# Sixteen tiles of experts on TensorE: half-column products kept together, activation behind the branch, transposes moved

## The chip, the cores and the metric

The kernel runs on one core of a Trainium2 chip. A core has TensorE (PE, with its weight loads listed as PEld), VectorE (DVE), ScalarE (ACT), GpSimd (POOL) and SyncE (SP), which run side by side and wait for each other through semaphores, and 16 DMA engines. The metric is the device time of one execution in microseconds (us).

## The reference, cut to what matters

Two blocks of a network, one after the other, on 512 tokens of width 1024. The change lies in the expert layer of the first block. 32 experts of inner width 256 stand in four groups; each token picks one group and two experts in it, with weights that come from softmaxes:

```python
for grp in range(N_GROUPS):
    sl = slice(grp * EXPERTS_PER_GROUP, (grp + 1) * EXPERTS_PER_GROUP)
    hg = jnp.einsum("td,edf->tef", ht, w_gate[sl])
    hu = jnp.einsum("td,edf->tef", ht, w_up[sl])
    act = jax.nn.silu(hg) * hu * combine[:, sl, None]
    y = y + jnp.einsum("tef,efd->td", act, w_down[sl])
```

All is in float32. The kernel computes an expert only for the tokens that picked it.

## The kernel before, in words

Before the experts, a router on the chip builds a table: 16 main tiles of 128 token places, each shared by two experts (number x and x + 16). One expert of a tile has its tokens in the first rows, the other in the last. Each has 64 rows of its own, and up to 32 more rows where it has more tokens; the flag `need[x]` says that such rows are in use in tile x. So a tile has *wide* products (64 rows for each expert, always) and *narrow* products (32 rows, under a branch on `need`).

For one tile x these steps are done (names as in the code and in the trace):

- `gather` (POOL): an indirect DMA fetches the 128 tokens' rows into `xg`; ACT scales them (`scale`, one ACTIVATE of 1,024 columns).
- `moe_xt`: 8 transposes on TensorE into two `pxt` banks, which DVE copies to `xt`.
- up: for k = 0..7 a product `moe_up` with each expert's `gu` weights, into the PSUM banks `pgA` and `pgB`. A wide product takes 64 columns of the array, and the two experts' products run at once in the two halves of the array. A float32 product shows as two matmul records in the trace, so that one k-step is two pairs of records.
- `narrow`: under a branch, the same products for the 32 more rows; in the other arm of the branch a product with a tile of zeros fills these rows.
- `moe_act`: four pieces, each a Silu on ACT and then a multiply on DVE, into `sa` and `sb`.
- `moe_st`: 4 transposes into the bank `pst`, and a DVE copy to `st`.
- `moe_down`: products of `st` with the `dn` weights into two banks `py`, again on half columns: part 0, a branch with the narrow rows, part 1. ACT copies the result rounded to `yh`, DVE subtracts for the rest, `yl`.
- `moe_hot` (DVE): `toh`, which has a one where a tile's place belongs to a token.
- `moe_back`: 8 banks `pb`, each filled by two products on full columns (`yh`, `yl` by `toh`), which return the rows to the tokens; DVE adds each bank to the residual `xT`.

The steps are skewed over the loop's iterations and stand in an order written by hand. Iteration x runs the up products of tile x; between its k-steps stand `moe_st` of tile x - 1 (behind k = 1) and the eight `moe_back` of tile x - 2 (one behind each of k = 1 to 6, two behind k = 7). Then come `narrow` and `moe_act` of x, `moe_xt` and `scale` for the next tiles, `moe_down` of x - 1, `moe_hot`, and the requests for weights. The banks `pxt`, `pst`, `py` and `pb` share a ring of four.

Weights come by SP's queue: `gu` of four transfers of 1,024 KB for each tile and `dn` of four of 512 KB. `pump`, at the end of iteration x, requests `dn` of tile x + 1 and `gu` of tile x + 3, whose buffers must be free; the rings hold three tiles of `gu` and two of `dn`.

A branch (`tc.If`) with no other arm, as in `moe_down` (L1880), is on TensorE's sequencer a COMPARE_BRANCH and, where it isn't taken, an EVENT_SEMAPHORE that does the semaphore counts that the products would have done. Behind the 16 main tiles a loop does further tiles of overfull experts.

Of the kernel before, what the change touches and what calls it, by code (L numbers as in the profile page):

```python
# [10 lines left out]
F32 = mybir.dt.float32  # L11
# [10 lines left out]
P = 128  # L22
T = 512
D = 1024
KD = 8
# [150 lines left out]
class Build:  # L176
# [1689 lines left out]
        self.nc.vector.tensor_copy(st[:, 0:2 * n], pt[:, 0:2 * n * P].rearrange("p (k t) -> p k t", t=P))  # L1866
        return st

    def moe_down(self, mp, st, dn, wide, narrow=(), need=None):


        pys = [self.pc("py") for _ in dn]

        def part(k, parts, start, stop):
            for py, d in zip(pys, dn):
                for i, r, n in parts:
                    self.mm(py[r:r + n], st[:, 2 * i + k, r:r + n], d[i][:, k, :], start, stop)
        part(0, wide, True, False)
        if narrow:
            with self.tc.If(need > 0):  # L1880
                for k in range(2):
                    part(k, narrow, False, False)
        part(1, wide, False, True)
        ys = []
        for py in pys:
            yh, yl = [mp.tile([P, T], F32R, tag="y", bufs=4, name=n) for n in ("yh", "yl")]
            self.act(yh, py, AF.Copy)
            self.tt(yl, py, yh.bitcast(F32), OP.subtract)
            ys.append((yh, yl))
        return ys  # L1890
# [67 lines left out]
    def moe(self, mp, pump, tab_d):  # L1958

        tab, ids = self.tab, self.ids  # L1960
        n = NMAIN
        rows = ((slice(0, 64), slice(64, 96)), (slice(32, 64), slice(64, 128))), ((slice(0, 32), slice(64, 128)), (slice(0, 64), slice(96, 128)))

        parts = ((((0, 0, 64), (1, 64, 64)), ((0, 64, 32), (1, 32, 32))), (((1, 0, 64), (0, 64, 64)), ((0, 0, 32), (1, 96, 32))))
        g, xt, ps, s, st, y, oh, need = {}, {}, {}, {}, {}, {}, {}, {}

        def scale(x):
            if x < n:
                self.act(g[x], g[x], AF.Copy, scale=tab[:, 3, x:x + 1])

        def start(x):
            if x == 0:
                scale(x)
            xt[x] = self.moe_xt(mp, g.pop(x))
            if x + 3 < n:
                g[x + 3] = self.gather(ids[:, x + 3:x + 4], x + 3)
            need[x] = self.nc.tensor.value_load(self.need[0:1, x:x + 1])
            ps[x] = [self.pd("pgA"), self.pd("pgB") if x % 2 == 0 else self.ps.tile([P, T], F32, tag="a", bufs=self.ps_a, name="pgB")]

        def narrow(x):  # L1980

            with self.tc.If(need[x] > 0) as c:
                for k in range(KD):
                    self.moe_up(ps[x], xt[x], gus, k, parts[x % 2][1])
            with c.Else():
                for i, r, m in parts[x % 2][1]:
                    self.mm(ps[x][i][r:r + m, :], self.zero[:, 0:m], self.zero)

        for x in range(3):
            g[x] = self.gather(ids[:, x:x + 1], x)  # L1990
        pump(0, 0, eng="gpsimd")
        start(0)
        scale(1)
        for x in range(n + 2):
            gus = [self.gus[x + 16 * i] for i in range(2)] if x < n else None
            for k in range(KD):
                if x < n:
                    self.moe_up(ps[x], xt[x], gus, k, parts[x % 2][0])
                if k == 1 and 0 < x <= n:
                    st[x - 1] = self.moe_st(mp, s.pop(x - 1))  # L2000
                for j in ((), range(k - 1, k), range(6, KD))[min(k, 1) + k // 7] if x > 1 else ():
                    self.moe_back(y[x - 2][j // 4], oh[x - 2], j // 4, (j % 4,))
            if x < n:
                narrow(x)
                i = x % 2
                s[x] = self.sA[i], self.sB[i]
                for e in range(2):
                    for r in rows[i][e]:
                        self.moe_act(s[x][e], ps[x][e], tab[:, 1 + e, x:x + 1], r)
                del ps[x], xt[x]  # L2010
            if x + 1 < n:
                start(x + 1)
            if x + 2 < n:
                scale(x + 2)
            if x == 0:
                self.route_extra([mp.tile([P, T], F32, tag="y", bufs=4, name="xs") for _ in range(4)])
            if x == 1:
                self.route_extra2()
                self.dma("scalar", tab_d, tab)
            if 0 < x <= n:  # L2020
                c = x - 1
                y[c] = self.moe_down(mp, st.pop(c), [[self.dns[c + 16 * e, h] for e in range(2)] for h in range(2)],
                                     *parts[c % 2], need[c])
                oh[c] = self.moe_hot(tab[:, 0, c:c + 1])
            pump(2 * (x + 1), 4 * x)

    def moe_extra(self, mp, mw, wg, wu, wd, tab_d, gu_bufs, dn_bufs):
# [773 lines left out]
```

## Time and profile before

| | |
|---|---|
| median of three runs | 2750.66 us (2750.01 to 2764.87) |
| profiled execution: its own time | 2758.55 us |
| profiled execution: span from the first to the last instruction | 2756.8 us |
| TensorE busy (whole span) | 2525.0 us, 92% |
| DVE, ACT, POOL busy (whole span) | 56%, 34%, 35% |
| main tiles of experts, first transposes to last `pb` | 780.7 to 1122 us |

The busy shares are of the whole execution; the experts are an eighth of it. What a change there does is read from the stretch itself. Times of single instructions are in us from the span's start. "[0.19 <-X]" behind an instruction is the idle time of its engine before it and what ended that. [...]

### The profile page before, as it was taken

How to read it: one execution, taken by the hardware profiler on the slowest of the kernel's cores; microseconds unless marked ns; L12 is line 12 of the kernel's file. 1: busy time of each engine (PE TensorE's matmuls, PEld its weight loads, DVE VectorE, ACT ScalarE, POOL GpSimd, SP SyncE). 2: the span in 40 equal slices, each digit the busy share in tenths (PEclk: the TensorE clock that was granted, in tenths of full speed). 3: DMA queues.
4: the chain of work that ended last, by engine and by line, in shares of the span. 5: the costliest groups of instructions: out<-in, count | busy, mean ns of one | idle time of the engine just before them, and what ended most of it. 6: DMA issues, size and time to landing. Idle time of an engine off the chain costs nothing.

```text
span 2756.8 us, 35101 instructions
## 1 busy us (share of the span) xinstructions
PE 2525.0 (92%) x13640; PEld 1836.8 (67%) x13640; DVE 1530.1 (56%) x2483; ACT 932.7 (34%) x1534; POOL 959.9 (35%) x652
## 2 busy tenths in 40 slices
PE   7887888787969999889999999999999999999999
PEld 4676776565533333557777777878756777888887
DVE  4896594344356645565465487884444345453523
ACT  3434223443212211333444332323332344442422
POOL 1454454333210000343553333344232343344443
PEclk8999998788979999999999999999999999999999
DMA  9356565634388974332445246552231225132321
GB/s 263 96 179 183 158 178 178 205 103 157 128 310 333 360 286 153 122 119 93 156 149 192 68 153 198 168 183 92 89 105 40 92 74 193 64 106 92 107 89 65
DMA packets 332300, 419.09 MB, mean 152 GB/s; under 512 B 33608, under 2 KB 275760, under 8 KB 323680
## 3 DMA queue, kind: packets, MB, share of 16 engines
q1 hardware_dynamic: 312848, 377.12, 41.6%
q10 hardware_dynamic: 14624, 25.28, 2.8%
q0 software_dynamic: 4656, 14.35, 1.6%
q8 instruction: 114, 1.87, 0.3%
q14 instruction: 58, 0.48, 0.1%
HBM read 387.66 MB, written 33.23 MB: 153 GB/s over the span
## 4 chain that ended last, share of the span: by engine, by line
PE 45%; DVE 6%; issue 3%; ACT 2%; POOL 2%; DMA 2%; ACTq 0%; POOLq 0%; DVEq 0%
PE pd L199 36%; PE psc L199 2%; DVE adacc L214 2%; PE tm L199 2%; POOL wlo L205 2%; PE ptot L199 1%; DMA raw<-in_w_up 1%; DVE cv L214 1%; PE po L199 1%; PE pc L199 1%; PE pz L199 1%; PE pso L199 1%; PE pst L199 1%; PE pn L199 1%; PE pr L199 1%
## 5 line engine op out<-in xcount | busy, mean ns | idle before, releaser
L205 POOL TENSOR_TENSOR wlo<-raw,whi 128x1024 fp32r<-128x1024 f32 (+3 forms) x317 | 721.0, 2280 | 1232.8 <-ACT whi L196 1208.9
L199 PE MATMUL pd<-h,whi 128*128 128x512 f32 (+1 forms) x3440 | 1099.4, 401 | 27.8 <-DVE stg L214 5.9
L199 PEld LDWEIGHTS pd<-h,whi 128*128 128x128 f32 x3440 | 647.4, 194 | 185.9 <-issue 26.1
L199 PE MATMUL pd<-h,wlo 128*128 128x512 f32 (+1 forms) x1720 | 676.1, 393 | 20.4 <-POOL wlo L205 20.4
L196 ACT ACTIVATE whi<-raw 128x1024 fp32r<-128x1024 f32 (+3 forms) x319 | 313.9, 993 | 265.7 <-PE pd L199 117.4
L199 PEld LDWEIGHTS pd<-h,wlo 128*128 128x128 f32 x1720 | 332.4, 193 | 93.0 <-POOL wlo L205 24.7
L199 PE MATMUL pd<-fyh,whi 128*128 128x512 f32 (+1 forms) x546 | 205.5, 376 | 10.7 <-ACT whi L196 5.2
L214 DVE SCALAR_TENSOR_TENSOR cv<-pd,vec,cv 128x511 f32<-128x511 f32 (+1 forms) x176 | 131.7, 748 | 144.0 <-ACT cv L196 138.4
L199 PE MATMUL pd<-fyh,wlo 128*128 128x512 f32 (+1 forms) x546 | 203.1, 372 | 6.0 <-POOL wlo L205 6.0
L199 PE MATMUL pd<-fyl,whi 128*128 128x512 f32 (+1 forms) x546 | 202.3, 371 | 2.5 <-DVE fyl L205 2.5
L214 DVE SCALAR_TENSOR_TENSOR adacc<-raw,cs,adacc 128x256 f32<-128x256 f32 x288 | 198.9, 691 | 9.4
L199 PE MATMUL pgB<-gu,xt 128*64 128x512 f32 (+1 forms) x304 | 154.8, 617 | 3.0 <-DVE xt L205 3.0
L214 DVE SCALAR_TENSOR_TENSOR xTl<-pd,mod,xTl 128x512 f32<-128x512 f32 (+1 forms) x73 | 49.4, 683 | 193.6 <-PE pd L199 193.6
L199 PE MATMUL pgA<-gu,xt 128*64 128x512 f32 (+1 forms) x304 | 154.9, 618 | 0.0
L199 PE MATMUL tm<-whi,h 128*128 128x256 f32 x640 | 129.5, 295 | 7.9 <-ACT whi L196 7.9
L214 DVE SCALAR_TENSOR_TENSOR xT<-pb,mod,xT 128x512 f32<-128x512 f32 x128 | 93.4, 748 | 77.0 <-PE pb L199 77.0
L199 PEld LDWEIGHTS pd<-fyh,whi 128*128 128x128 f32 x546 | 105.4, 193 | 42.0 <-ACT whi L196 11.7
L199 PEld LDWEIGHTS pd<-fyh,wlo 128*128 128x128 f32 x546 | 105.3, 193 | 24.8 <-POOL wlo L205 7.7
L199 PEld LDWEIGHTS pd<-fyl,whi 128*128 128x128 f32 x546 | 105.1, 192 | 19.5 <-DVE fyl L205 3.2
L199 PEld LDWEIGHTS tm<-whi,h 128*128 128x128 f32 x640 | 106.4, 199 | 9.2 <-ACT whi L196 8.4
L199 PE MATMUL tm<-wlo,h 128*128 128x256 f32 x320 | 93.5, 292 | 7.7 <-POOL wlo L205 7.6
L196 ACT ACTIVATE cv<-pd,vec 128x512 f32<-128x512 f32 x88 | 68.2, 775 | 95.3 <-PE pd L199 94.8
(564 smaller groups left out, 3383.4 us busy)
## 6 DMA issues: line engine op xcount, KB each, us to landing
raw<-in_ada SPq DMA_DIRECT2D x64, 1024.0 KB, 5.3
raw<-in_w_in SPq DMA_DIRECT2D x54, 1024.0 KB, 5.4
raw<-in_w_up SPq DMA_DIRECT2D x44, 1024.0 KB, 5.0
gu<-in_wg SPq DMA_DIRECT2D x30, 1024.0 KB, 8.5
gu<-in_wu SPq DMA_DIRECT2D x30, 1024.0 KB, 7.0
dn<-in_wd SPq DMA_DIRECT2D x59, 512.0 KB, 8.3
raw<-in_w_dn SPq DMA_DIRECT2D x16, 1024.0 KB, 5.2
raw<-in_wo SPq DMA_DIRECT2D x12, 1024.0 KB
```

Source lines behind the costliest of these rows:

```text
L196: return self.nc.scalar.activation(out, in_, func, **kw)
L199: return self.nc.tensor.matmul(out, lhsT, rhs, start=start, stop=stop)
L205: return (eng or self.nc.vector).tensor_tensor(out, a, b, op=op)
L214: return (eng or self.nc.vector).scalar_tensor_tensor(out, a, s, b, op0=op0, op1=op1)
```

## The change

Within an iteration the order is made anew. `moe_st` of tile x - 1 and the first four `moe_back` of tile x - 2 stand together behind k = 2. Behind k = 5 stand `moe_xt`, the gather and `scale` for the following tiles (`rows_of`), and then the other four `moe_back`. The up products of k = 6 and 7, part 0 of `moe_down` of x - 1, both branches, part 1, and the next tile's k = 0 to 2 follow each other with nothing on full columns between. The narrow up products and `moe_act` (`end_up`) are called between part 0 and the branch of `moe_down`. The branch of the up products has no other arm any more: four banks are taken once ahead of the loop, their narrow rows are filled with zeros once, and tiles of one parity use the same two banks. `moe_hot` stands ahead of `moe_down`. In the first two iterations the last pieces of the router's table (`route_extra`, `route_extra2`) are moved with it.

```diff
--- before.py
+++ after.py
@@ -1866,7 +1866,7 @@
         self.nc.vector.tensor_copy(st[:, 0:2 * n], pt[:, 0:2 * n * P].rearrange("p (k t) -> p k t", t=P))
         return st
 
-    def moe_down(self, mp, st, dn, wide, narrow=(), need=None):
+    def moe_down(self, mp, st, dn, wide, narrow=(), need=None, between=None):
 
 
         pys = [self.pc("py") for _ in dn]
@@ -1876,6 +1876,8 @@
                 for i, r, n in parts:
                     self.mm(py[r:r + n], st[:, 2 * i + k, r:r + n], d[i][:, k, :], start, stop)
         part(0, wide, True, False)
+        if between is not None:
+            between()
         if narrow:
             with self.tc.If(need > 0):
                 for k in range(2):
@@ -1968,60 +1970,62 @@
             if x < n:
                 self.act(g[x], g[x], AF.Copy, scale=tab[:, 3, x:x + 1])
 
-        def start(x):
-            if x == 0:
-                scale(x)
+        def rows_of(x):
             xt[x] = self.moe_xt(mp, g.pop(x))
             if x + 3 < n:
                 g[x + 3] = self.gather(ids[:, x + 3:x + 4], x + 3)
             need[x] = self.nc.tensor.value_load(self.need[0:1, x:x + 1])
-            ps[x] = [self.pd("pgA"), self.pd("pgB") if x % 2 == 0 else self.ps.tile([P, T], F32, tag="a", bufs=self.ps_a, name="pgB")]
-
-        def narrow(x):
-
-            with self.tc.If(need[x] > 0) as c:
+
+        def end_up(x):
+
+            with self.tc.If(need[x] > 0):
                 for k in range(KD):
                     self.moe_up(ps[x], xt[x], gus, k, parts[x % 2][1])
-            with c.Else():
-                for i, r, m in parts[x % 2][1]:
-                    self.mm(ps[x][i][r:r + m, :], self.zero[:, 0:m], self.zero)
+            i = x % 2
+            s[x] = self.sA[i], self.sB[i]
+            for e in range(2):
+                for r in rows[i][e]:
+                    self.moe_act(s[x][e], ps[x][e], tab[:, 1 + e, x:x + 1], r)
+            del ps[x], xt[x]
 
         for x in range(3):
             g[x] = self.gather(ids[:, x:x + 1], x)
         pump(0, 0, eng="gpsimd")
-        start(0)
+
+        banks = [[self.pd("pgA"), self.pd("pgB")], [self.pd("pgA"), self.ps.tile([P, T], F32, tag="a", bufs=self.ps_a, name="pgB")]]
+        for x in range(2):
+            for i, r, m in parts[x][1]:
+                self.mm(banks[x][i][r:r + m, :], self.zero[:, 0:m], self.zero)
+        scale(0)
+        rows_of(0)
         scale(1)
         for x in range(n + 2):
             gus = [self.gus[x + 16 * i] for i in range(2)] if x < n else None
+            if x < n:
+                ps[x] = banks[x % 2]
+
             for k in range(KD):
                 if x < n:
                     self.moe_up(ps[x], xt[x], gus, k, parts[x % 2][0])
-                if k == 1 and 0 < x <= n:
+                if k == 2 and 0 < x <= n:
                     st[x - 1] = self.moe_st(mp, s.pop(x - 1))
-                for j in ((), range(k - 1, k), range(6, KD))[min(k, 1) + k // 7] if x > 1 else ():
-                    self.moe_back(y[x - 2][j // 4], oh[x - 2], j // 4, (j % 4,))
-            if x < n:
-                narrow(x)
-                i = x % 2
-                s[x] = self.sA[i], self.sB[i]
-                for e in range(2):
-                    for r in rows[i][e]:
-                        self.moe_act(s[x][e], ps[x][e], tab[:, 1 + e, x:x + 1], r)
-                del ps[x], xt[x]
-            if x + 1 < n:
-                start(x + 1)
-            if x + 2 < n:
-                scale(x + 2)
+                if k == 5 and x + 1 < n:
+                    rows_of(x + 1)
+                    scale(x + 2)
+                    if x == 1:
+                        self.route_extra2()
+                        self.dma("scalar", tab_d, tab)
+                if k in (2, 5) and x > 1:
+                    self.moe_back(y[x - 2][k // 5], oh[x - 2], k // 5, range(4))
+            if 0 < x <= n:
+                c = x - 1
+                oh[c] = self.moe_hot(tab[:, 0, c:c + 1])
+                y[c] = self.moe_down(mp, st.pop(c), [[self.dns[c + 16 * e, h] for e in range(2)] for h in range(2)],
+                                     *parts[c % 2], need[c], (lambda: end_up(x)) if x < n else None)
+            elif x == 0:
+                end_up(0)
             if x == 0:
                 self.route_extra([mp.tile([P, T], F32, tag="y", bufs=4, name="xs") for _ in range(4)])
-            if x == 1:
-                self.route_extra2()
-                self.dma("scalar", tab_d, tab)
-            if 0 < x <= n:
-                c = x - 1
-                y[c] = self.moe_down(mp, st.pop(c), [[self.dns[c + 16 * e, h] for e in range(2)] for h in range(2)],
-                                     *parts[c % 2], need[c])
-                oh[c] = self.moe_hot(tab[:, 0, c:c + 1])
             pump(2 * (x + 1), 4 * x)
 
     def moe_extra(self, mp, mw, wg, wu, wd, tab_d, gu_bufs, dn_bufs):
```

## Rows read from the trace of the kernel before

**Rows 1.** One steady tile (busy of each engine, PEclk, DMA share, GB/s).

```profile
846.73:865.48 18.75, 18.56 (x80) 6.94 (x78) 11.40 (x20) 3.85 (x7) 0.99 (x1) 1.00 0.92 348
```

**Rows 2.** Waits from 780 to 1130 us (us in total, times, longest).

```profile
PE pb L199 <- DVE toh L210: 4.4, 3, 1.9
```

**Rows 3.** Timeline of PE, one tile (start, us, instructions, idle before).

```profile
845.85 0.39 PE L199 MATMUL pb<-toh,yh 128*128 128x512 f32 x1
846.08 0.40 PE L199 MATMUL pb<-toh,yl 128*128 128x512 f32 x1
...
846.73 1.16 PE L202 MATMUL pxt<-const_ident,xg 128*128 128x128 f32 x8
847.82 1.94 PE L199 MATMUL py<-dn,st 128*64 128x512 f32 x8
849.94 1.94 PE L199 MATMUL py<-dn,st 128*64 128x512 f32 x8 [0.19 <-PE py L199]
851.68 0.59 PE L199 MATMUL pgA<-gu,xt 128*64 128x512 f32 x1
...
853.53 0.51 PE L202 MATMUL pst<-const_ident,sa 128*128 128x128 f32 x2
...
854.03 0.48 PE L199 MATMUL pb<-toh,yh 128*128 128x512 f32 x1
...
854.67 0.64 PE L199 MATMUL pgA<-gu,xt 128*64 128x512 f32 x1
...
856.35 0.64 PE L199 MATMUL pgA<-gu,xt 128*64 128x512 f32 x1
...
865.48 1.16 PE L202 MATMUL pxt<-const_ident,xg 128*128 128x128 f32 x8
```

**Rows 4.** The branch L1880, 846 to 852 us (ns min/median/max, starts).

```profile
L1880 PEldq COMPARE_BRANCH  x1: 207/207/207, 847.5 to 847.5; - x1
L1880 PEldq EVENT_SEMAPHORE  x1: 51/51/51, 849.8 to 849.8; - x1
```

**Rows 5.** The branch L1880, 809 to 812 us.

```profile
L1880 PEldq COMPARE_BRANCH  x1: 213/213/213, 809.7 to 809.7; - x1
L1880 PEldq EVENT_SEMAPHORE  x1: 51/51/51, 810.9 to 810.9; - x1
```

**Rows 6.** Timeline of ACT and DVE, the same tile as in rows 3.

```profile
846.05 1.41 DVE L214 SCALAR_TENSOR_TENSOR xT<-pb,mod,xT 128x512 f32<-128x512 f32 x2 [0.92 <-PE pb L199]
...
846.83 0.37 ACT L196 ACTIVATE sa<-pgA 32x256 f32<-32x256 f32 x1 [13.01 <-PE pgB L199]
...
849.71 0.49 DVE L214 SCALAR_TENSOR_TENSOR sb<-sb,tab,pgB 32x256 f32<-32x256 f32 x1 [0.44 <-ACT sb L196]
...
851.75 0.69 DVE L205 TENSOR_TENSOR yl<-py,yh 128x512 fp32r<-128x512 f32 x1 [0.23 <-ACT yh L196]
```

**Rows 7.** Timeline of ACT, the scaling of tile 3.

```profile
811.24 1.15 ACT L196 ACTIVATE xg<-xg,tab 128x1024 f32<-128x1024 f32 x1 [2.80 <-DMA xg<-xa_d,ids]
```

**Rows 8.** Timeline of PE: first products of tiles 1 to 3.

```profile
795.82 0.64 PE L199 MATMUL pgB<-gu,xt 128*64 128x512 f32 x1 [2.96 <-DVE xt L205]
...
812.75 0.59 PE L199 MATMUL pgA<-gu,xt 128*64 128x512 f32 x1
...
832.92 0.59 PE L199 MATMUL pgB<-gu,xt 128*64 128x512 f32 x1
```

**Rows 9.** A stretch of the second tile (columns as in rows 1).

```profile
796.00:799.50 3.50, 3.50 (x10) 1.19 (x10) 2.19 (x5) 0.00 (x0) 0.85 (x1) 0.55 1.00 405
```

**Rows 10.** Timeline of PE, the end of the main tiles.

```profile
1104.40 0.47 PE L199 MATMUL pb<-toh,yh 128*128 128x512 f32 x1 [1.28 <-DVE toh L210]
...
1117.86 0.47 PE L199 MATMUL pb<-toh,yh 128*128 128x512 f32 x1 [1.91 <-DVE toh L210]
```

**Rows 11.** DMA queues, 846.73 to 865.48 us (packets, MB, share of 16 engines).

```profile
q8 instruction: 1, 0.02, 0.3%
```

**Rows 12.** The tile xg from 840 to 1010 us.

```profile
DMA to landing us min/median/max: 4.3/4.7/5.9
```

## The prediction, made blind

> **What bounds the kernel now.** I read first where the change lies, then the view of stretches: a steady tile takes 18.75 us, TensorE is busy 18.56 us of it at the full clock, and VectorE, the next, 11.4 us [rows 1]. The list of waits over the experts shows hardly anything that TensorE waits for: what is largest there belongs to the first and the last tiles [rows 2]. So the steady tile is bound by TensorE's own stream, and the question is what in 18.75 us isn't product. The timeline of TensorE answers that [rows 3]. Eight records of `py` (four pairs) run from 849.94 to 851.68: 1.74 us, 0.43 us a pair. Full-column products follow each other every 0.23 us (845.85, 846.08). But from 854.67 to 856.35, two pairs with one `pb` between (two full products), pass 1.68 us, where 2 x 0.43 + 2 x 0.23 is 1.33 us. **One excursion from half columns to full ones and back costs 0.35 us**, and nobody is waited for. Before, there are eight such excursions in a tile: `pst` with the first `pb`, five single `pb`, the last two `pb`, and `pxt`, which the zero products part from them.
>
> **The change, part by part.**
>
> *Fewer excursions.* After, there are two: `pst` with four `pb`, `pxt` with four `pb`. Five fewer in the k-loop give 5 x 0.35 = 1.75 us. The sixth vanishes with the zero products: from the last `pb` product to the transposes now pass 846.08 to 846.73, 0.65 us, where two full-column instructions would be 0.23 us apart [rows 3]; 0.42 us. Together -2.17 us for each tile.
>
> *The branch.* Where `moe_down`'s branch isn't taken, its two parts start 847.82 and 849.94, 2.12 us apart where four pairs take 1.74: a hole of 0.38 us. Its COMPARE_BRANCH ran at 847.5, over two microseconds ahead of the products, so the branch itself is free; what costs is the EVENT_SEMAPHORE, which stands until 849.8, when part 0 is done and TensorE has run empty [rows 4]. The old up branch has no such hole, since the zero products in its other arm do the counting. Now both branches are of the costly kind, but they stand side by side, so TensorE empties once. New is that the second COMPARE_BRANCH can run only behind the first EVENT_SEMAPHORE, with nothing queued: 0.207 us, its own EVENT_SEMAPHORE 0.051 us, and again some 0.2 us of handing over (the first product stood 0.1 us behind the event, twice that to be safe). I take +0.45 us, an estimate from rows 4. Below: 0, if the sequencer gets past it in time. Above: at 809.7 a branch ended (with its 213 ns) at 809.95 and the event behind it stood at 810.9 [rows 5], so that finding the target took at most 0.95 us; 0.21 + 0.95 + 0.05 is 1.2 us. I stay near the low end, since the event of rows 5 is explained by products that ended about then. [...]
>
> So a tile takes 18.75 - 2.17 + 0.45 = 17.03 us, 1.7 us less.
>
> *What must stay hidden for that.* The activation chain (four Silu and four multiplies) took from 846.83 to 850.20, 3.4 us [rows 6]. It now starts at the first event; to the transposes of `pst` pass the second branch, part 1 (1.74) and three k-steps (2.6), 4.8 us. Slack 1.4 us. `yl` of the first bank then follows about 0.9 us behind the chain (`yh` waits for ACT, then 0.69 us), and its reader, the first `pb`, stands 0.5 us behind `pst`: slack 1 us. Four `pb` in a row fill in 4 x 0.47 us while VectorE empties one in 0.66 (two took 1.41 together) [rows 6]: each new `pb` needs the bank of four uses earlier. The nearest are the fourth `pb`, which needs the copy of `pst`, and the last two, which need the copies of `pxt`: a slack of 0.2 to 0.45 us. If these miss, a tile pays up to 0.5 us. All are positive, so I cost them at nothing.
>
> *Weights and gathers.* The requests for weights still stand behind `moe_down`; gathers are issued some 34 us before their scaling and land after 5.9 us at most in the steady part [rows 12]. Moved past each other on ACT: `scale` of a later tile now stands ahead of `moe_act`, so a late gather would hold the activations. That happens once, in the head.
>
> *The head.* TensorE stood 2.96 us before tile 1's products [rows 8], until VectorE had done the activations and then `xt`; with the transposes behind k = 5 this goes. But the gather of tile 3 lands only at 811.24, where ACT had waited 2.80 us for it [rows 7]; it stands behind weights in the queue, and these don't change. In the new order ACT has to scale tile 3 (to 812.4) before it may activate tile 1, whose chain then ends at 815.8. The transposes of tile 1 wait for it, where TensorE would come at about 811. [...] From 815.8 the rest of that tile is 17.0 - 2.7 = 14.3 us, plus 1.6: tile 3 starts at 831.7 instead of 832.92 [rows 8]. Gain 1.2 us; without the late gather 7 us, at worst 0.
>
> *The tail.* In the last tile five excursions are saved and no zero products (its narrow rows are used, as are those of two others): 1.75 us. The wait of 1.28 us for `toh` turns into one for the activation chain, which is no longer covered; that of 1.91 us goes to about 0.9, since `toh` comes first now [rows 10]. Together 2.7 us.
>
> *Sum.* Tiles 3 to 15: 12 x 1.7 = 20.4 us. With head and tail 24.3 us. All that follows the experts waits for their last sum, so it moves up whole. Profiled execution: 2758.55 - 24 = 2734.5 us. The median of before lies 7.9 us under the profiled time; I take the same difference from it: **2726.5 us**.
>
> **The rivals.**
>
> *The second branch is dear.* At 1.2 us for each of 13 tiles, 0.75 us more than taken: +10 us, 2736. For it: no row shows a branch that TensorE runs into empty. Against it: rows 4 and 5 bound it.
>
> *The transfers bind.* A tile moves 18.75 us x 348 GB/s = 6.5 MB at a busy share of 0.92 [rows 1]. If that share can't be packed more tightly than to 1.0, a tile needs 17.3 us, and 12 x 0.25 = 3 us are lost: 2730. If the rate can't rise at all, only head and tail remain: 2747. Against it: 405 GB/s in rows 9, at which 6.5 MB take 16.1 us; and loads are requested two tiles ahead.
>
> *The activation becomes the wait.* If the activations are released only behind part 1, 2.2 us later, `pst` waits 0.8 us and the first `pb` 0.4 us more in each tile: +1.2 x 13, 2742. For it: the slack is the smallest of the long chains. Against: the event does the counting that ACT waits for.
>
> *Nothing gained.* The excursions' 0.35 us might be bound to the counts of products, not to the switches; then 2.17 us shrink to the zero products' 0.42, which the branch eats, and some 2 us of head and tail remain: 2748. Against it: the same products in a row at 0.23 and 0.43 us.
>
> *Slower: a fetch behind the second branch.* Instructions come by DMA, one packet of 0.02 MB in a tile [rows 11], in the same engines as the weights. A jump that TensorE meets empty can't hide such a fetch as it did at 847.5. If one is needed and queues behind weights for, say, 5 us in every tile (the gathers' landing in rows 12 shows what a small transfer takes there), 13 x (5 - 0.45) = 59 us: 2786. It eats the gain of 24 us from 1.9 us a tile beyond what I took, and is slower by over 0.5% from 2.9 us. [...] Against it: one packet serves about a whole tile, the jump passes only the skipped narrow products, and rows 5 show a target found within 0.95 us.
>
> **How the numbers follow.** My forecast, 0.66 (own range 2717 to 2734: branch at 0 gives 2720.5, the head without its wait 2720.5, both 2714.5; banks missed by 0.5 us, 2733). Dear branch 0.10, transfers 0.05, activation 0.07, nothing gained 0.06, fetch 0.06. Half a per cent, 13.75 us, is about what a measurement of this kernel can tell from no change: faster ends at 2737. The forecast, the dear branch, and most of the transfers are faster: 0.80; activation, nothing gained and the rest same: 0.14; the fetch slower: 0.06. The range 2716 to 2740 leaves out the fetch, the activation, nothing gained and the ends of the forecast.
>
> **What would show it.** Right: steady tiles of about 17 us; no zero products in the loop; two excursions in a tile; both events side by side with one hole of about 0.8 us before part 1; no wait at `pst` or `pb` in steady tiles; a wait of some 4 us at tile 1's `pst` for the scaling of tile 3, then half clock; DMA near 380 GB/s. Wrong: a hole of over 1.2 us at the branches, `pst` waiting for `sb` or `pb` for `xT` in every tile, products waiting for `gu`, or pairs and full products that take longer in a row than now.

## The result, and the profile after

| | before | after |
|---|---|---|
| median of four runs each | 2751.94 us (2750.01 to 2764.87) | 2725.45 us (2719.16 to 2728.39) |
| profiled execution | 2758.55 us | 2728.39 us |
| first transposes of the experts | 780.66 | 783.15 |
| first product of tile 3 | 832.92 | 833.93 |
| first product of tile 15 | 1077.91 | 1056.83 |
| end of the last sum into `xT` | 1123.96 | 1100.15 |

The ratio is 0.9881 (95% interval 0.986 to 0.9901): 1.2% faster, more than twice the half per cent that the prediction took for no change. The forecast of 2726.5 us is 1 us away from the median.

The rows of the table say where it comes from. From the first transposes to the last sum the experts took 343.3 us and now take 317.0: 26.3 us less. Of these, 1.5 us lie ahead of tile 3's products (52.26 to 50.78), 22.1 us in tiles 3 to 14 (244.99 to 222.90), and 2.7 us behind (46.05 to 43.32). The code behind the experts is unchanged, and so is that ahead of them but for the zero fills of the banks; still the experts began 2.5 us later, and what follows them took 6.4 us less. Such stretches scatter: over the ten kernels of this study the first transposes stand between 780.3 and 793.1, and what follows the last sum takes 1620.1 to 1632.8 us. A single steady tile, however, repeats to 0.1 us or better, so the causes below are read from tiles, and the whole times are only a check on the sum.

The view of stretches for two steady tiles, from one tile's `pst` to the next, with the columns of [rows 1] (start and end, us, busy time and count of instructions of PE, PEld, DVE, ACT and POOL, the clock granted to TensorE as a share of its full speed, the busy share of the DMA engines, GB/s):

```profile
853.56:870.49 16.93, 16.33 (x79) 7.67 (x77) 10.84 (x18) 3.63 (x7) 0.99 (x1) 1.00 0.99 376
870.49:887.41 16.92, 16.32 (x78) 7.66 (x76) 10.85 (x18) 3.62 (x7) 0.99 (x1) 1.00 1.00 384
```

A tile takes 16.93 us where it took 18.75. TensorE is still the engine that is busy nearly throughout, at the full clock; the DMA engines' busy share has gone from 0.92 to 0.99 and the rate from 348 to about 380 GB/s [rows 1]. The timeline of TensorE through the first of these tiles answers to [rows 3]:

```profile
846.63 1.89 PE L199 MATMUL py<-dn,st 128*64 128x512 f32 x8
849.12 1.94 PE L199 MATMUL py<-dn,st 128*64 128x512 f32 x8 [0.60 <-PEq L1882]
850.86 0.59 PE L199 MATMUL pgA<-gu,xt 128*64 128x512 f32 x1
...
853.56 0.51 PE L202 MATMUL pst<-const_ident,sa 128*128 128x128 f32 x2
...
854.06 0.48 PE L199 MATMUL pb<-toh,yh 128*128 128x512 f32 x1
...
855.77 0.40 PE L199 MATMUL pb<-toh,yl 128*128 128x512 f32 x1
856.10 0.64 PE L199 MATMUL pgA<-gu,xt 128*64 128x512 f32 x1
...
858.83 1.16 PE L202 MATMUL pxt<-const_ident,xg 128*128 128x128 f32 x8
859.74 0.48 PE L199 MATMUL pb<-toh,yh 128*128 128x512 f32 x1
...
861.79 0.64 PE L199 MATMUL pgA<-gu,xt 128*64 128x512 f32 x1
...
870.49 0.50 PE L202 MATMUL pst<-const_ident,sa 128*128 128x128 f32 x2
```

There are two excursions, 853.56 to 856.10 and 858.83 to 861.79, none with a wait in brackets. The zero products are gone, and the products of the next tile follow part 1 of `py` at once. The one bracket in the tile is the hole between the two parts of `py`: they start 2.49 us apart, where they were 2.12 apart [rows 3]. TensorE's sequencer around that hole, as a list by line (which instruction, its duration in ns, its start), answers to [rows 4]:

```profile
L1981 PEldq EVENT_SEMAPHORE  x1: 51/51/51, 848.6 to 848.6; - x1
L1882 PEldq COMPARE_BRANCH  x1: 208/208/208, 848.7 to 848.7; - x1
L1882 PEldq EVENT_SEMAPHORE  x1: 51/51/51, 849.0 to 849.0; - x1
```

The first event stands until part 0 is done, at 848.6. Only then does the second branch run, 208 ns with nothing queued behind it, and its event comes 0.3 us after its start, so that finding the target took some 0.1 us.

TensorE's list of waits over the experts (for what, us in total, times, the longest one) answers to [rows 2]:

```profile
PE py L199 <- PEq L1882: 6.6, 13, 0.6
...
PE pst L202 <- DVE sa L214: 2.4, 1, 2.4
PE pst L202 <- DVE sb L214: 1.6, 2, 0.9
```

The first line is the branch, 13 times 0.5. `pst` waits only in the head, twice, and once in the last tile; no line names `gu`, so no product waits for weights.

The head, on ScalarE's timeline:

```profile
812.79 1.15 ACT L196 ACTIVATE xg<-xg,tab 128x1024 f32<-128x1024 f32 x1 [14.55 <-DMA xg<-xa_d,ids]
...
813.96 0.37 ACT L196 ACTIVATE sa<-pgA 32x256 f32<-32x256 f32 x1
```

and on TensorE's:

```profile
815.91 0.47 PE L202 MATMUL pst<-const_ident,sa 128*128 128x128 f32 x2 [2.35 <-DVE sa L214]
...
817.26 0.70 PE L202 MATMUL pst<-const_ident,sb 128*128 128x128 f32 x2 [0.87 <-DVE sb L214]
...
824.98 1.16 PE L202 MATMUL pxt<-const_ident,xg 128*128 128x128 f32 x8
...
833.93 0.59 PE L199 MATMUL pgB<-gu,xt 128*64 128x512 f32 x1
```

The gather of tile 3 is late, ScalarE waits for it, and the activation of tile 1 stands behind. Behind the two waits comes a stretch at the low clock:

```profile
813.00:818.00 5.00, 1.78 (x9) 0.93 (x5) 2.58 (x6) 3.73 (x8) 0.00 (x0) 0.84 0.96 293
818.00:823.00 5.00, 5.00 (x12) 2.68 (x13) 4.04 (x7) 0.83 (x1) 0.00 (x0) 0.50 1.05 427
823.00:828.00 5.00, 5.00 (x28) 2.84 (x26) 2.27 (x4) 0.00 (x0) 0.99 (x1) 0.98 1.00 419
```

From 818 to 823 the granted clock is 0.50, with 12 instructions where the next 5 us hold 28; full-column products start 0.43 us apart there (818.67, 819.10, 819.53), where a steady tile has 0.23.

The tail, on TensorE's timeline of the last tile:

```profile
1079.56 0.50 PE L202 MATMUL pst<-const_ident,sa 128*128 128x128 f32 x2
1080.84 0.51 PE L202 MATMUL pst<-const_ident,sb 128*128 128x128 f32 x2 [0.77 <-DVE sb L214]
...
1086.15 7.36 PE L199 MATMUL py<-dn,st 128*64 128x512 f32 x32
...
1093.44 0.49 PE L199 MATMUL pb<-toh,yh 128*128 128x512 f32 x1
```

The waits of 1.28 and 1.91 us for `toh` in front of `pb` [rows 10] are gone; 0.77 us for the last activation has come. By milestones, from the first product of tile 15: its `pst` comes 1.74 us sooner (24.47 to 22.73), which is five excursions; from there to the last `py` it takes 0.38 us longer (6.21 to 6.59); and from there to the last sum 1.37 us less (15.37 to 14.00). So the wait of 1.28 us gave nothing back: the eight returns behind it go at the pace of VectorE's additions (seven in 4.69 us), which begin 3.16 us behind `pst` (1082.72) where they began 2.76 behind it (1105.14).

### The profile page after: what moved, and what is told of

It is laid out like the page before. It is cut to its first block, busy times and chain, and to the rows that moved or that the text cites. A ratio compares the mean times of both kernels' runs of the same rounds, so it can differ in the third digit from the quotient of the medians.

```text
span 2726.6 us, 35040 instructions
## 1 busy us (share of the span) xinstructions
PE 2490.4 (91%) x13618; PEld 1843.4 (68%) x13618; DVE 1524.1 (56%) x2483; ACT 929.5 (34%) x1534; POOL 957.9 (35%) x652
## 4 chain that ended last, share of the span: by engine, by line
PE 45%; DVE 6%; issue 3%; POOL 2%; ACT 2%; DMA 1%; ACTq 0%; POOLq 0%; DVEq 0%
PE pd L199 36%; PE psc L199 2%; DVE adacc L214 2%; PE tm L199 2%; POOL wlo L205 2%; PE ptot L199 1%; DMA raw<-in_w_up 1%; DVE cv L214 1%; PE po L199 1%; DVE h L214 1%; PE prr L199 1%; PE pc L199 1%; PE pz L199 1%; PE pso L199 1%; PE pst L199 1%
## 5 line engine op out<-in xcount | busy, mean ns | idle before, releaser
L199 PE MATMUL pgB<-gu,xt 128*64 128x512 f32 (+1 forms) x304 | 143.1, 608 | 0.3 <-PEq L1981 0.3
L199 PE MATMUL pgA<-gu,xt 128*64 128x512 f32 (+1 forms) x304 | 143.2, 608 | 0.0
L214 DVE SCALAR_TENSOR_TENSOR xT<-pb,mod,xT 128x512 f32<-128x512 f32 x128 | 87.0, 742 | 2.1 <-PE pb L199 1.9
```

The lines of the kernel that those rows point to most:

```text
L199: return self.nc.tensor.matmul(out, lhsT, rhs, start=start, stop=stop)
L214: return (eng or self.nc.vector).scalar_tensor_tensor(out, a, s, b, op0=op0, op1=op1)
```

## The experiments

All are made from the changed kernel, and run beside the kernel before (2760.21 us beside e1, e3, e4 and e5, 2763.06 beside the others). "Tile" is the time from one steady tile's `pst` to the next, "experts" that from the first transposes to the last sum. The column "by the ratio" is the ratio less 0.9881, times 2751.94 us, and has an uncertainty of 7 to 11 us; "by the experts" is the stretch less 317.0 us.

| kernel | ratio to before (95%) | tile | experts | by the experts | by the ratio |
|---|---|---|---|---|---|
| after | 0.9881 (0.986, 0.9901) | 16.93 | 317.0 | | |
| e1_spread | 0.9934 (0.9915, 0.9954) | 18.31 | 335.8 | +18.8 | +14.6 |
| e2_pairs | 0.9921 (0.99, 0.9942) | 17.60 | 326.9 | +9.9 | +11.0 |
| e3_scale_late | 0.9854 (0.9823, 0.9886) | 16.93 | 310.9 | -6.1 | -7.4 |
| e4_apart | 0.9877 (0.9842, 0.9912) | 17.01 | 314.6 | -2.4 | -1.1 |
| e5_zeros | 0.9902 (0.9871, 0.9932) | 16.83 | 315.1 | -1.9 | +5.8 |
| e6_no_branch | 0.973 (0.9711, 0.975) | 16.11 | 276.3 | -40.7 | -41.6 |
| e7_both | 0.9852 (0.9835, 0.9869) | 16.82 | 309.1 | -7.9 | -8.0 |
| e8_one | 0.989 (0.987, 0.991) | 17.17 | 313.2 | -3.8 | +2.5 |

The two columns agree within that uncertainty; that they are equal to 0.1 us for e7 is chance. For e5 and e8 they have opposite signs: there the whole time can't say more than that the change is small. Differences of a few microseconds between these kernels are shown by the stretches of one execution each, not by the ratios.

**Six excursions instead of two.** The activation, the branches and the transposes stay where the change put them; only the returns are spread again, one behind each of k = 2 to 6 and three behind k = 7.

```diff
-                if k in (2, 5) and x > 1:
-                    self.moe_back(y[x - 2][k // 5], oh[x - 2], k // 5, range(4))
+                if k > 1 and x > 1:
+                    for j in (k - 2,) if k < 7 else (5, 6, 7):
+                        self.moe_back(y[x - 2][j // 4], oh[x - 2], j // 4, (j % 4,))
```

> The changed kernel with the eight returns (moe_back) spread over the k-steps again: one behind each of k = 2 to 6, three behind k = 7; nothing else. Excursions to full columns: six in a tile instead of two, the same number of products. If a switch of columns costs 0.35 us for the way there and back, a steady tile takes 16.93 + 4 x 0.35 = 18.3 us, and 14 tiles 19.6 us more: 2745. Rival: the cost hangs on the products and not on the switches; then a tile stays at 16.9 us and the time at 2725.

TensorE's timeline, the first transposes of two tiles in a row:

```profile
871.10 0.51 PE L202 MATMUL pst<-const_ident,sa 128*128 128x128 f32 x2
...
889.41 0.51 PE L202 MATMUL pst<-const_ident,sa 128*128 128x128 f32 x2
```

18.31 us a tile, 1.38 more for four more excursions: 0.345 us each, with the same products. Three quarters of the gain of a tile (1.38 of 1.82) is the count of excursions and nothing else; had they cost nothing, this kernel would have stayed at 16.93.

**Four excursions.** Two returns behind each of k = 2, 3, 5 and 6.

```diff
-                if k in (2, 5) and x > 1:
-                    self.moe_back(y[x - 2][k // 5], oh[x - 2], k // 5, range(4))
+                if k in (2, 3, 5, 6) and x > 1:
+                    j = (2, 3, 5, 6).index(k)
+                    self.moe_back(y[x - 2][j // 2], oh[x - 2], j // 2, range(2 * (j % 2), 2 * (j % 2) + 2))
```

> The changed kernel with the eight returns two by two behind k = 2, 3, 5 and 6: four excursions in a tile, between the two of the changed kernel (16.93 us) and the six of the spread kernel (18.31 us). If each excursion costs the same 0.35 us, a steady tile takes 16.93 + 2 x 0.345 = 17.62 us. Rival: what counts is that VectorE empties the banks beside half-column products, which two by two already gives; then 16.9 us.

The same two rows of TensorE's timeline:

```profile
873.42 0.50 PE L202 MATMUL pst<-const_ident,sa 128*128 128x128 f32 x2
...
891.02 0.50 PE L202 MATMUL pst<-const_ident,sa 128*128 128x128 f32 x2
```

17.60 us: 0.67 for two, 0.335 each. The cost is linear in the count, at two, four and six.

**The scaling behind the activation.** `scale` of tile x + 2 goes from behind k = 5 to the end of the iteration, so that on ScalarE a late gather holds no activation.

```diff
                 if k == 5 and x + 1 < n:
                     rows_of(x + 1)
-                    scale(x + 2)
...
+            if x + 2 < n:
+                scale(x + 2)
             pump(2 * (x + 1), 4 * x)
```

> The changed kernel with scale(x + 2) at the end of an iteration, behind the activations and the copies of py on ACT, as in the kernel before; nothing else. If tile 1's transposes waited 2.35 and 0.87 us because the late gather of tile 3 stood ahead of the activations on ACT, both waits go, and with them the products at half clock behind (8.2 us from pst to pxt, less the 0.9 us waited, against 5.3 in a steady tile, some 2.9 us): 6 us less, 2719.5. Rival: VectorE, busy with the last pieces of the router's table there, would hold the activations anyway; then under 1.5 us less.

ScalarE's timeline in the head:

```profile
817.04 0.37 ACT L196 ACTIVATE sa<-pgA 32x256 f32<-32x256 f32 x1 [9.21 <-PEq L1981]
...
821.59 1.15 ACT L196 ACTIVATE xg<-xg,tab 128x1024 f32<-128x1024 f32 x1
```

and TensorE's:

```profile
821.92 0.51 PE L202 MATMUL pst<-const_ident,sa 128*128 128x128 f32 x2
822.27 0.40 PE L202 MATMUL pst<-const_ident,sb 128*128 128x128 f32 x2
```

The activation of tile 1 now waits for its products' count alone (the event of L1981), the scaling comes behind it, and `pst` has no wait. The experts are 6.1 us shorter, all in the head, where the times from `pst` to `pst` behind tiles 0 and 1 fall from 17.41 and 20.72 to 15.0 and 16.92; a steady tile is the same. From 805 to 841 every pair of up products in a row starts 0.43 us behind the one before and every full-column product of the returns 0.23, but for those next to a switch: nothing runs at half that pace any more. So the late gather, through ScalarE's order, is what the head paid for, with its clock.

**The branches apart.** The up branch and the activation go ahead of `moe_down`, so that part 0 stands between the two branches, where both stood behind it.

```diff
                 oh[c] = self.moe_hot(tab[:, 0, c:c + 1])
+                if x < n:
+                    end_up(x)
                 y[c] = self.moe_down(mp, st.pop(c), [[self.dns[c + 16 * e, h] for e in range(2)] for h in range(2)],
-                                     *parts[c % 2], need[c], (lambda: end_up(x)) if x < n else None)
+                                     *parts[c % 2], need[c])
```

> The changed kernel with the up branch and the activations ahead of part 0 of moe_down, so that the two branches stand apart with part 0 between; nothing else. The second of two branches side by side cost 0.37 us in a steady tile of the changed kernel (a gap of 2.49 us from part 0 to part 1 instead of 2.12), a branch by itself 0.38. If each is one hole of its own, it makes no difference where they stand: a tile stays at 16.9 us and the time within 2 us of 2725.5. Rival: standing side by side spares an emptying of TensorE; then apart costs up to 0.4 us a tile, 5 us.

TensorE's timeline, the two parts of `py`:

```profile
867.52 1.94 PE L199 MATMUL py<-dn,st 128*64 128x512 f32 x8 [0.31 <-DVE toh L210]
869.62 1.94 PE L199 MATMUL py<-dn,st 128*64 128x512 f32 x8 [0.16 <-PEq L1882]
```

Each branch now has its own hole, and part 1 starts 2.10 us after part 0, as before the change (2.12, [rows 3]). The tile takes 17.01 us, 0.08 more. So putting the branches side by side saves next to nothing: two holes apart cost what one double hole costs, within 0.1 us. The bracket at part 0 names `toh`, which VectorE finished at 867.37, just behind the event of the up branch (867.3); so the 0.08 us may be a wait for `toh` and not the price of a second emptying. The 2.4 us that the experts are shorter don't come from the branches of steady tiles: the head gives 2.6 us (15.93 and 19.72 instead of 17.41 and 20.72, where the late gather of tile 3 is scaled 28.0 us behind the first transposes and not 29.6) and the tail 1.2, and the tiles between take 1.4 back.

**The zero products back.** The other arm of the up branch again does the counting with two products of zeros.

```diff
-            with self.tc.If(need[x] > 0):
+            with self.tc.If(need[x] > 0) as c:
                 for k in range(KD):
                     self.moe_up(ps[x], xt[x], gus, k, parts[x % 2][1])
+            with c.Else():
+                for i, r, m in parts[x % 2][1]:
+                    self.mm(ps[x][i][r:r + m, :], self.zero[:, 0:m], self.zero)
```

> The changed kernel with the products of zeros back in the other arm of the up branch; nothing else. They stand among products on half columns now, so they open no excursion of their own: a pair of 512 columns, some 0.2 us, and they do the semaphore counts, so that only moe_down's branch empties TensorE. If the second branch side by side costs 0.37 us, a tile gets 0.15 us shorter, 16.8 us, and the time 2 us less: 2723.5. Rival: the zeros' removal was itself a gain, as in the kernel before, where it was worth 0.42 us; then a tile gets longer by up to 0.4 us, 2731.

TensorE's timeline, the two parts of `py` and what stands between them:

```profile
872.54 1.89 PE L199 MATMUL py<-dn,st 128*64 128x512 f32 x8
874.36 0.39 PE L199 MATMUL pgA<-zero 128*32 128x512 bf16 x1
...
874.93 1.94 PE L199 MATMUL py<-dn,st 128*64 128x512 f32 x8 [0.18 <-PEq L1882]
```

The parts are 2.39 us apart instead of 2.49, and the tile takes 16.83 us, 0.10 less. Among products on half columns the zeros are the cheaper way to count: they take 0.27 us more than a lone branch (2.39 - 2.12; the 0.2 expected was an estimate, near the 0.23 between full-column products of 512 columns in [rows 3]), where they took 0.42 before [rows 3]. That the difference is the switch between them and the full-column products that stood beside them fits, but no run separates it. The first transposes of this execution stand at 792.53, 9.4 us later than in the one after the change, which is why its whole time says nothing of 0.10 us a tile.

**No branch at all.** Both branches and the narrow products under them are taken out.

```diff
         if between is not None:
             between()
-        if narrow:
-            with self.tc.If(need > 0):
-                for k in range(2):
-                    part(k, narrow, False, False)
         part(1, wide, False, True)
...
-            with self.tc.If(need[x] > 0):
-                for k in range(KD):
-                    self.moe_up(ps[x], xt[x], gus, k, parts[x % 2][1])
```

> The changed kernel without both branches and without the narrow products under them, so that tokens in the 32 more rows of an expert are left out of the sum. If the two holes cost 0.38 + 0.37 us, a steady tile takes 16.93 - 0.75 = 16.18 us, and the three tiles with narrow rows lose their 10 us each: 2725.5 - 10 - 31 = 2685. Rival: the transfers bind below 17 us; then a tile stays at 16.5 to 17.3 us and the products of the up step wait for gu.

The view of stretches, two steady tiles:

```profile
871.20:887.40 16.20, 16.20 (x78) 7.54 (x78) 11.03 (x19) 3.74 (x7) 1.09 (x2) 1.00 1.03 409
887.40:903.60 16.20, 16.20 (x78) 7.59 (x77) 11.04 (x19) 3.74 (x7) 1.08 (x2) 1.00 1.03 409
```

and TensorE's timeline, the transposes of tile 1 and the down products of a later tile:

```profile
828.99 0.67 PE L202 MATMUL pst<-const_ident,sa 128*128 128x128 f32 x2 [7.76 <-DVE sa L214]
...
873.83 3.60 PE L199 MATMUL py<-dn,st 128*64 128x512 f32 x16
```

Both parts of `py` are one unbroken row. The tile takes 16.11 us, 0.82 less (0.75 expected): the price of both branches together in a tile of the changed kernel. The transfers follow, at 409 GB/s, and no product of a steady tile waits for weights (TensorE's list of waits from 840 to 1000 us is empty); they aren't the bound at 16.93. Most of the 40.7 us by which the experts are shorter is work left out in the three tiles whose narrow rows are used. The longer wait in the head, 7.76 us, is the late gather again, met earlier.

**The two useful edits together.** The scaling late, the zero products back, and the first zero fill of the banks, which the other arm then does, removed. The diffs are those of the third and fifth experiments, and

```diff
-        for x in range(2):
-            for i, r, m in parts[x][1]:
-                self.mm(banks[x][i][r:r + m, :], self.zero[:, 0:m], self.zero)
```

> The changed kernel with both edits that the stretches of single tiles favour: scale(x + 2) at the end of an iteration (the experts took 310.9 us with it alone, 317.0 without), and the products of zeros in the other arm of the up branch (16.83 us a tile instead of 16.93). If they add up, the experts take 310.9 - 12 x 0.1 = 309.7 us and the time is 7 us under the changed kernel's, some 2718. Rival: the zeros let the activations wait for one more product, and the head loses it again; then 311 to 313 us.

The view of stretches, one steady tile:

```profile
845.44:862.26 16.82, 16.64 (x80) 7.76 (x78) 10.85 (x19) 3.62 (x8) 0.99 (x1) 1.00 1.01 383
```

The experts take 309.06 us, 7.9 less than after the change, and the whole has a ratio of 0.9852 (0.9835 to 0.9869) to the kernel before. By the stretch it is the best version of the study, and the parts add up (6.1 in the head, 0.1 in each tile, 0.6 more than that in all); by the ratio it can't be told from e3 (0.9854).

**One excursion.** The same kernel with `pxt`, `pst` and all eight returns behind k = 4.

```diff
-                if k == 5 and x + 1 < n:
+                if k == 4 and x + 1 < n:
                     rows_of(x + 1)
...
-                if k == 2 and 0 < x <= n:
+                if k == 4 and 0 < x <= n:
                     st[x - 1] = self.moe_st(mp, s.pop(x - 1))
...
-                if k in (2, 5) and x > 1:
-                    self.moe_back(y[x - 2][k // 5], oh[x - 2], k // 5, range(4))
+                if k == 4 and x > 1:
+                    for h in range(2):
+                        self.moe_back(y[x - 2][h], oh[x - 2], h, range(4))
```

> The kernel with both edits (scaling late, zeros in the other arm) and one excursion instead of two: behind k = 4 the eight transposes of pxt, the four of pst and all eight returns. One switch less is worth 0.35 us: 16.83 - 0.35 = 16.48 us if nothing waits. But eight banks in a row are emptied by VectorE at 0.66 us each where TensorE fills one in 0.47, behind three other copies in the same ring of four banks: I expect the last three returns to wait 0.5 us in all, 17.0 us a tile, so that two excursions are the better number.

TensorE's timeline, the last four returns of a tile and the next tile's transposes:

```profile
872.42 0.50 PE L199 MATMUL pb<-toh,yh 128*128 128x512 f32 x1
...
873.08 0.49 PE L199 MATMUL pb<-toh,yh 128*128 128x512 f32 x1
...
873.74 0.50 PE L199 MATMUL pb<-toh,yh 128*128 128x512 f32 x1
...
874.39 0.50 PE L199 MATMUL pb<-toh,yh 128*128 128x512 f32 x1
...
887.23 0.40 PE L202 MATMUL pst<-const_ident,sa 128*128 128x128 f32 x2
```

and VectorE's, the eight additions:

```profile
871.62 5.35 DVE L214 SCALAR_TENSOR_TENSOR xT<-pb,mod,xT 128x512 f32<-128x512 f32 x8
```

One excursion less should give 16.82 - 0.345 = 16.48 us; the tile takes 17.17. From the fifth on, the returns come 0.66 us apart, where four in a row came 0.47 apart after the change: VectorE empties a bank in 5.35 / 8 = 0.67 us, and with a ring of four a return needs the bank of four uses earlier. That is 0.69 us in a tile, more than the 0.5 expected. Four returns in a row cost no wait, eight do; no run stands between.

## Why the prediction was right

*What binds.* TensorE's own stream did, as read: taking switches out of it shortened the tile by what they cost, and nothing else came to light behind it down to 16.11 us. With the sizes that were measured, 5 x 0.345 + 0.42 - 0.37 is 1.78 of the 1.82 us.

*The excursions.* 0.35 us each was worked out from one record pair [rows 3]; two experiments, with the same products, measured 0.345 and 0.335, there and back. The timeline of TensorE before shows where it lies, around one single `pb` (the next pair starts at 856.35 [rows 3]):

```profile
855.15 0.59 PE L199 MATMUL pgA<-gu,xt 128*64 128x512 f32 x1
...
855.68 0.50 PE L199 MATMUL pb<-toh,yh 128*128 128x512 f32 x1
856.02 0.40 PE L199 MATMUL pb<-toh,yl 128*128 128x512 f32 x1
...
856.83 0.59 PE L199 MATMUL pgA<-gu,xt 128*64 128x512 f32 x1
```

Against 0.43 us for a pair and 0.23 for a full product, each switch comes 0.10 us late (0.53 and 0.33), the second full product another 0.11 (0.34) and the second pair 0.05 (0.48). So nearly half of the price comes behind the switches themselves; why, no run separates.

*The branch.* +0.45 us was taken, between 0 and 1.2; +0.37 was measured (2.49 - 2.12). The second branch met TensorE empty, as said, and its parts are those of the estimate: 0.21, 0.05 and some 0.1 of handing over, where 0.2 was taken. What was wrong is the thought that standing side by side saves something: the second branch costs 0.37 us, the lone one had a hole of 0.38 [rows 3], and apart they cost at most 0.08 more.

*The zero products.* Their 0.42 us were credited to their removal. They need not have gone: among half columns zeros are 0.10 us cheaper than the branch that replaced them. The sum isn't hurt, since removal and branch were costed together, -0.42 + 0.45; the reading of what to remove is.

*The tile and the cover.* 17.03 us predicted, 16.93 measured. The slacks (1.4, 1 and 0.2 to 0.45 us) all held: no bracket at `pst` or `pb` in a steady tile. The last experiment shows the price where eight returns in a row use up the smallest, 0.69 us.

*The head.* A gain of 1.2 us was predicted and 1.5 measured, by two errors that cancel. The waits were 2.35 + 0.87 = 3.2 us, not 4.8 (815.8 - 811): the gather came 1.55 us later, but the experts 2.5, and the transposes of `sa` could begin ahead of `sb`. The clock cost more: from `pst` to `pxt` passed 9.07 us, where a steady tile takes 5.27 (853.56 to 858.83); 0.87 is the second wait, and 2.9 us are lost to the clock, not 1.6. The 1.6 us in the sum is 3.5 x 0.45, from a granted clock of 0.55 for 3.5 us before [rows 9]; no run shows that term in the new order, where the clock stood at 0.50 for 5.5 us (817.62 to 823.13). That the late gather is the cause was argued ahead, and the third experiment shows it.

*The tail.* 2.7 us predicted and measured, again by two errors that cancel. The excursions gave their 1.75 us (1.74). The wait for the activation chain was to cost what that for `toh` had; with it VectorE's additions begin later, and 0.38 us are lost. The second wait for `toh` was to give 1.0 us back; 1.37 came.

*The sum.* 24 us predicted in the experts, 26.3 measured: 22.1 instead of 20.4 in the twelve tiles (0.12 us in each, and 0.1 more in each of the two with narrow rows), the rest in the head. "All that follows moves up whole" can't be seen to better than the scatter of some 13 us, and the profiled execution gained 30.2, of which 3.9 lie outside the experts. That the median came out within 1 us is partly luck; the 26 us are not.

*The rivals.* A dear branch: 0.37 us, with the next event 0.3 us behind the branch. The transfers: about 380 GB/s in a tile, and 409 where TensorE allowed it. The activation: no wait at `pst` in a steady tile. Nothing gained: excluded by the count of excursions alone. A fetch behind the second branch: no hole behind it was longer than 0.6 us, in any of the 13 tiles. That a jump may have to wait for a fetch was a supposition, and no run shows one that did; these jumps pass the few narrow products, and a farther one was not tried.

## What to carry to other kernels

Where an engine is busy all the time, price the order of its stream as well as its instructions: compare the distance of two kinds in a row with that where they alternate, and group them as far as the banks between engines allow: here four in a row cost no wait, and eight did. When a step is moved past another on the same engine (here ScalarE, where the activation began at 813.96, behind the scaling of 812.79), look for the one late arrival among its inputs; here a single gather in the head cost 6 us until the scaling was put behind the work that others wait for. A change that is worth 1% of a whole program is read from the stretch that it touches, since the unchanged stretches scattered here by some 13 us, on either side of it.

## What the runs showed of the hardware

- A branch that isn't taken and has no other arm costs TensorE some 0.4 us (0.38 before [rows 3], 0.37 behind another branch), also where the branch itself ran two microseconds ahead: the event that does its counts started at 849.8 [rows 4], when the products ahead of it were done (847.82 + 1.94 = 849.76 [rows 3]). Both of a tile's branches cost 0.82 us; zeros in the other arm of one gave back 0.10.
- A COMPARE_BRANCH that wasn't taken into the narrow products took 0.207 us in a busy TensorE [rows 4] and 0.208 in an empty one, and its event followed 0.3 us behind its start: no run shows a price of the jump beyond that.
- The DMA engines moved 409 GB/s over whole tiles, at a busy share of 1.03, beside a TensorE that never waited (e6_no_branch); at a share of 0.92 [rows 1] the queue was not yet the bound.
- Waits of 2.35 and 0.87 us were followed by 5 us at a granted clock of 0.50, and the clock cost about as much as the waits (2.9 and 3.2 us).
